# Weight slots, shared row buffers and PSUM banks in the expert stage of a hybrid decoder block

## Chip, cores and metric

The kernel runs on one NeuronCore of a Trainium2 chip. The metric is the device time of one execution in microseconds (us). What is compared are medians over several executions; lower is better.

## What is computed

One decoder block over 512 tokens of width 1024, all in float32. First comes a mixer (attention with a window, and a gated linear recurrence), then a mixture of experts, then a last norm. The change touches the expert stage alone. Cut to that stage, the reference does this:

```
logits = h @ w_router + b_router                  # 512 tokens, 32 experts
top_vals, top_idx = top_k(logits, 4); gates = softmax(top_vals)
for each expert e, for the tokens xb that chose it:
    gu   = xb @ w_gu[e] + b_gu[e]                 # 1024 -> 2 x 1024
    gate = min(gu[:, :1024], 7); up = clip(gu[:, 1024:], -7, 7)
    y    = ((up + 1) * gate * sigmoid(1.702 * gate)) @ w_down[e] + b_down[e]
    out[token] += y * gates[token, e]
```

There are 2048 pairs of a token and an expert, spread unevenly: an expert may have a few rows or some three hundred. The weights of one expert are 12 MB (8 MB of w_gu, 4 MB of w_down), 384 MB in all, and each is read from DRAM once.

## The kernel before

**Weights.** An expert's weights are loaded in 12 chunks of 1 MB, 8 of w_gu and then 4 of w_down, by SyncE's queue (`load`, L1115, issues at L1119 and L1123). A chunk lives in a slot of 128 x 2048 float32. `ORDER` (L1099) lists 20 slots; slot 19 is not among them, since it holds three other tiles (below). `pump` (L1129) issues loads while there are free slots. The 8 slots of w_gu come free when the gate and up products of that expert are done (`used(e, False)`), the 4 of w_down after its down products (`used(e, True)`). `paced` (L1105) keeps at most 4 loads under way. Before the first expert starts 18 chunks are asked for (`pump(KD + 4 + EARLY)`), and the rest of the slots are filled during the first expert.

**Experts.** One pass of the loop over e at the end of the function does, in the order of the program: the gate and up products of e (`gate_up`), the turning of the token rows of e+1 (`turn_x`, L1158), the gather of the rows of e+2 (`gather`, L1084), and the down products of e-1 (`down`). Rows are taken in tiles of 32 tokens; a tile of gate and up products is 64 matmul instructions (L1195), a tile of down products 64 (L1218). Up to four tiles are one block, and `nest` (L1166) skips tiles that an expert doesn't have, by branches on the expert's count. Experts with over 128 rows run `further`, for blocks 1 to 3.

**Down products and output.** A tile of down products goes into a PSUM bank given by `pd` (L1140), banks 4 and 5 by turns for block 0. `put` (L1221) then adds the bias (L1224, from `bd_` or for further blocks `bdx`, which `bias2` fills at L931), scales by the gate (L1225) into a row buffer `Y[:, t]`, four buffers for four tiles, and GpSimd scatters it with addition into the result in DRAM (L1226, 128 rows of 256 float32, an indirect DMA of the software queue).

**Picking rows.** For expert e+2 a one-hot tile `T_HOT` is made on VectorE (L951) right after the output of e-1, and TensorE multiplies by it between the second and the third chunk of the next gate and up products (L1068, the first step of `between`). VectorE, TensorE and GpSimd each work strictly in their own order.

**Buffers around the change.** Slot 19 holds `a4[5]` (the rows `XR` of a further block) and `a4[6]` (`bdx` in its first quarter, `T_HOT` in its second half). `a4[4]` holds `HX`, the activations of a further block, `a4[3]` the four buffers `Y`.

```
pg = lambda b, t: pall[:, 2 + t % 2 if b else t, :]
pd = lambda b, t: pall[:, (0 if b else 4) + t % 2, 0:256]
def put(e, b, t):
    si, f = INFO[e, b // 2]
    y = Y[:, t]
    V.tensor_tensor(y, pd(b, t), bdx if b else bd_, op=OP.add)
```

Of the kernel before, what the change touches and what calls it, by code (L numbers as in the profile page):

```python
# [13 lines left out]
OP = mybir.AluOpType  # L14
# [26 lines left out]
def block_kernel(ctx, tc, x, c, w_ada, b_ada, g_mix, w_in, conv_w, conv_b, w_rg_a, b_rg_a, w_rg_x,  # L41
# [3 lines left out]
    V, A, PE, G = nc.vector, nc.scalar, nc.tensor, nc.gpsimd  # L45
# [12 lines left out]
    pall = psp.tile([128, 8, 512], FT, name="pall")  # L58
# [34 lines left out]
    a4 = [wk.tile([128, D], FT, name=f"a{i}") for i in range(NA4)]  # L93
# [61 lines left out]
    btg = keep.tile([128, 768], FT, name="btg")  # L155
# [574 lines left out]
    def run_all(g):  # L730
        for _ in g:
            pass
# [182 lines left out]
    def new(name, tag=None):  # L915
        shape, dt, bufs = KINDS[name]
        return wk.tile(shape, dt, name=name, tag=tag or name, bufs=1 if tag else bufs)

    def hot_tile(at):
        return at[:, :NT * 128].bitcast(BF).rearrange("p (t n) -> p t n", t=NT)  # L920

    bd_ = wk.tile([128, 256], FT, name="bd")
    T_HOT = hot_tile(a4[6][:, 512:])
    BG = new("bg")


    def bias(e):
        V.stream_shuffle(BG, btg[:, :512], [e] * 32)  # L928

    def bias2(e, dst=bd_):  # L930
        V.stream_shuffle(dst, btg[:, 512:], [e] * 32)  # L931

    for tb in range(NT):
        assemble(tb, 0)
# [15 lines left out]
    def hot(oh, e, c, tb):  # L950
        V.tensor_scalar(oh[:, tb], slots, 256.0 * c, posm[:, tb, e:e + 1], op0=OP.add, op1=OP.is_equal)  # L951
# [86 lines left out]
    part = lambda i: a4[i].rearrange("p (t n) -> p t n", t=4)  # L1038
# [3 lines left out]
    def prep(e, c, oh, own=None, bk=5, tbs=range(NT)):  # L1042
        mk = (lambda n: own[n]) if own else new
        for tb in tbs:
            hot(oh, e, c, tb)
        yield
        where(e, c, oh, mk, bk)
        yield
        yield from spots(e, c, mk)

    def spots(e, c, mk):
        p, g1 = INFO[e, c]
        PE.matmul(p[:, 16:56], rep, g1.rearrange("p b t c -> p (b t c)"), start=True, stop=True)  # L1053
        p2 = p[:, 16:56].rearrange("p (b t c) -> p b t c", b=2, t=4)
        f, si = mk("f"), mk("si")
        V.tensor_copy(f[:, 0], p2[:, :, :, 1])  # L1056
        V.scalar_tensor_tensor(si, p2[:, :, :, 0], jcol, f[:, 0], op0=OP.add, op1=OP.add)
        V.tensor_copy(f[:, 1], p2[:, :, :, 3])
        V.tensor_tensor(f[:, 1], f[:, 1], p2[:, :, :, 2], op=OP.add)
        V.tensor_tensor(f[:, 1], f[:, 1], p2[:, :, :, 4], op=OP.add)  # L1060
        INFO[e, c] = (si, f)
        yield

    def where(e, c, oh, mk, bk):
        p = pall[:, bk, 0:56]
        for b in range(2):
            for tb in range(NT):
                PE.matmul(p[:, 5 * b:5 * b + 5], oh[:, tb, 128 * b:128 * b + 128], vals[:, tb, e, :],  # L1068
                          start=(tb == 0), stop=(tb == NT - 1))
        p3 = p[:, 0:10].rearrange("p (b c) -> p b c", b=2)  # L1070
        i1 = mk("i1")
        gi = GI[e, c] = mk("gi")
        V.tensor_reduce(i1, p3[:, :, 0:2], axis=AX.X, op=OP.add)
        V.tensor_scalar(gi, i1, 0.25, 1024.0, op0=OP.mult, op1=OP.add)
        g1 = mk("g1")
        V.tensor_tensor(g1, p3[:, :, None, :].to_broadcast([128, 2, 4, 5]),
                        tmask[:, None, :, None].to_broadcast([128, 2, 4, 5]), op=OP.mult)
        INFO[e, c] = (p, g1)

    def gather(e, b, x_, reg=None):  # L1080
        XROW[e, b] = x_

        def rows(p0, p1):
            G.indirect_dma_start(out=x_[p0:p1], out_offset=None, in_=h2_d,  # L1084
                                 in_offset=bass.IndirectOffsetOnAxis(
                                     ap=GI[e, b // 2][p0:p1, b % 2:b % 2 + 1], axis=0),
                                 bounds_check=S - 1, oob_is_err=False)

        if reg is None:
            return rows(0, 128)  # L1090
        with tc.If(reg > 128 * b + 64) as cmp:  # L1091
            rows(0, 128)
        with cmp.Else():
            with tc.If(reg > 128 * b + 32) as small:
                rows(0, 64)
            with small.Else():
                rows(0, 32)

    ORDER = (17, 14, 7, 12, 18, 11, 15, 13, 10, 9, 6, 2, 3, 4, 5, 16, 0, 8, 1, 20)  # L1099
    WG, WD = {e: [] for e in range(NE)}, {e: [] for e in range(NE)}  # L1100
    HELD, free, paces = {}, list(ORDER), []
    todo = [(e, k) for e in range(NE) for k in range(KD + 4)]
# [34 lines left out]

    pg = lambda b, t: pall[:, 2 + t % 2 if b else t, :]

    pd = lambda b, t: pall[:, (0 if b else 4) + t % 2, 0:256]  # L1140


    def xpose(e, b, xT):
        turn_x(e, b, xT)
        scale_x(e, b, xT, 0, 4)
# [68 lines left out]
    def dn(e, b, ht, t):  # L1214
        w = WD[e]
        for k in range(KD):
            for j in range(4):
                PE.matmul(pd(b, t)[32 * j:32 * j + 32], ht[:, t, 32 * k:32 * k + 32], w[k][:, j],  # L1218
                          start=(k == 0), stop=(k == KD - 1), tile_position=(0, 32 * j))

    def put(e, b, t):  # L1221
        si, f = INFO[e, b // 2]
        y = Y[:, t]
        V.tensor_tensor(y, pd(b, t), bdx if b else bd_, op=OP.add)  # L1224
        V.scalar_tensor_tensor(y, y, f[:, 1, b % 2, t:t + 1], gt2, op0=OP.mult, op1=OP.mult)  # L1225
        st = G.indirect_dma_start(out=x1_d, out_offset=bass.IndirectOffsetOnAxis(ap=si[:, b % 2, t:t + 1], axis=0),  # L1226
                                  in_=y, in_offset=None, bounds_check=S * 4 - 1, oob_is_err=False,
                                  compute_op=OP.add)
        tc.declare_no_dep(st.ins, group=f"sc{e}", reason="an expert's slots have rows of their own")
        tc.add_to_no_dep_group(f"sc{e}", st.ins)  # L1230


    H = [part(0), part(2)]
    TU, Y, HX, XR, bdx = part(1), part(3), part(4), a4[5], a4[6][:, :256]

    def gate_up(e, r, between):
        def tile(t):
# [12 lines left out]
    def down(e, r):  # L1250
        def tile(t):
            dn(e, 0, H[e % 2], t)
            put(e, 0, t)

        tile(0)
        nest(r, 0, tile, None, f"d{e}")


    def further(e, r):
        own = {n: new(n, n + "x") for n in ("g1", "i1", "gi", "f", "si")}  # L1260

        def products(t):
            gu(e, b, t)
            act(e, b, HX, t)

        def sums(t):
            dn(e, b, HX, t)
            put(e, b, t)

        def block():  # L1270
            xpose(e, b, XT[e, 0])
            if b < 3:
                with tc.If(r > 128 * b + 128):
                    if b == 1:
                        run_all(prep(e, 1, T_HOT, own, 1))
                    gather(e, b + 1, XR)
            products(0)
            nest(r, b, products)
            sums(0)
            nest(r, b, sums)  # L1280

        bias2(e, bdx)
        b = 1
        block()
        with tc.If(r > 256):
            b = 2
            block()
            with tc.If(r > 384):
                b = 3
                block()  # L1290

    pump(KD + 4 + EARLY)
# [6 lines left out]
    def second_rows(e):  # L1299
        with tc.If(G.value_load(cnt[0:1, e:e + 1], min_val=0, max_val=S) > 128):  # L1300
            gather(e, 1, XR)

    for e in range(NE):
        r = rn
        if e:
            second_rows(e)
            bias2(e - 1)
        prs = [prep(e + 2, 0, T_HOT)] if e + 2 < NE else []
        if e == 0:
            prs = [prep(u, 0, OH[u], None, bk, ()) for u, bk in ((1, 5), (0, 7), (2, 4))]  # L1310
        for pr in prs:
            next(pr)
        if e == 0:
            gates_of()

        def between():
            for pr in prs:
                next(pr, None)
            if e == 0 and (1, 0) not in XROW:
                gather(1, 0, xg)  # L1320
                second_rows(0)

                nc.sync.value_load(xg.bitcast(I32)[0:1, 0:1])
                pump()

        gate_up(e, r, between)
        used(e, False)
        if e:
            hint(rp, 32, f"d{e - 1}", 1)
        for pr in prs:  # L1330
            run_all(pr)
        if e + 1 < NE:
            rn = count(e + 1)
            bias(e + 1)
            turn_x(e + 1, 0, new("xT"))
            scale_x(e + 1, 0, XT[e + 1, 0], 0, 4)
        if e + 2 < NE:
            gather(e + 2, 0, xg, G.value_load(cnt[0:1, e + 2:e + 3], min_val=0, max_val=S))  # L1338
        if e:
            down(e - 1, rp)  # L1340
            used(e - 1, True)
        rp = r
# [59 lines left out]
```

## Time and profile before

| what | value |
|---|---|
| median of 3 runs | 1523.88 us (1520.62 to 1529.71) |
| the profiled execution, its own time | 1519.37 us |
| its span in the profile | 1517.5 us |
| TensorE matmul busy | 1226.6 us, 81% of the span |
| VectorE busy | 617.5 us, 41% |
| bytes moved by DMA | 473.02 MB, mean 312 GB/s |
| mean granted TensorE clock | 0.926 of full speed |

The rows of the prediction come from one execution, so its sums are made against 1519.37 us; that lies 4.5 us below the median. The expert stage runs from 257 us to 1495 us of the span. No engine and no queue is busy throughout: shares over the whole span say little, and what counts is which of two chains (TensorE's order, or the stream of weights) ends last in a given stretch.

### The profile page before, as it was taken

What the parts mean: (1) busy time and instruction counts of PE and PEld (TensorE: products, weight loads), DVE (VectorE), ACT (ScalarE), POOL (GpSimd) and SP (SyncE); (2) the same over time, 40 slices, a digit from 0 to 9 for tenths busy, and PEclk for the clock granted to TensorE, in tenths of its full rate; (3) what the DMA queues carried; (4) which work ended last, traced back from release to release, by engine and by line L of the source; (5) the groups of instructions that cost most, each with busy time, mean ns of one, the idle gap of its engine ahead of it and who ended that gap; (6) DMA issues with size and microseconds to landing.
All of it is one profiled execution on the core that took longest, in us unless ns stands there. A gap on an engine that the chain in (4) does not pass through costs nothing. (4 is left out here: it accounts for less than half of the span.)

```text
span 1517.5 us, 32068 instructions
## 1 busy us (share of the span) xinstructions
PE 1226.6 (81%) x12297; PEld 541.8 (36%) x12297; DVE 617.5 (41%) x1687; ACT 210.3 (14%) x467; POOL 264.1 (17%) x224
## 2 busy tenths in 40 slices
PE   6998979678888988789777688798858887879782
PEld 4655657222332433223212322352412242233331
DVE  4738856424344333333323323433422343324323
ACT  3445524100100010000000000000000000000001
POOL 3305731100120012101100200110200031011102
PEclk9998999999999999989878988999978999999997
DMA  9973158897996039989998988897998899579963
GB/s 325 334 281 102 56 233 327 352 379 306 399 388 250 10 88 406 384 337 400 391 398 330 395 360 339 310 388 305 398 394 311 364 392 405 209 286 347 401 263 124
DMA packets 94319, 473.02 MB, mean 312 GB/s; under 512 B 12888, under 2 KB 36652, under 8 KB 42764
## 3 DMA queue, kind: packets, MB, share of 16 engines
q1 hardware_dynamic: 76684, 447.39, 74.5%
q0 software_dynamic: 16928, 20.21, 6.0%
q8 instruction: 176, 2.88, 0.8%
q14 instruction: 179, 1.47, 0.2%
q10 hardware_dynamic: 352, 1.07, 0.2%
HBM read 457.78 MB, written 17.06 MB: 313 GB/s over the span
## 5 line engine op out<-in xcount | busy, mean ns | idle before, releaser
L1195 PE MATMUL pall<-wc,xT 128*32 128x512 f32 x5248 | 643.0, 635 | 131.2 <-DMA wc<-in_w_gu_dram 64.4
L1195 PEld LDWEIGHTS pall<-wc,xT 128*32 128x32 f32 x5248 | 166.3, 114 | 526.1 <-issue 414.4
L1218 PE MATMUL pall<-wc,a 128*32 128x256 f32 x5248 | 306.2, 389 | 34.2 <-DVE a L1224 19.1
L1218 PEld LDWEIGHTS pall<-wc,a 128*32 128x32 f32 x5248 | 176.0, 112 | 157.5 <-issue 29.4
L1226 POOL DMA_INDIRECT x_d<-a,si x82 | 128.2, 1563 | 409.7 <-DVE a L1225 259.0
L1206 ACT ACTIVATE a<-a 128x256 f32<-128x256 f32 x82 | 34.2, 417 | 916.0 <-DVE a L1205 916.0
L1203 DVE TENSOR_TENSOR a<-pall,bg 128x256 f32<-128x256 f32 x82 | 34.8, 425 | 275.7 <-PE pall L1195 275.7
L1084 POOL DMA_INDIRECT xg<-h_d,gi x31 | 33.0, 1064 | 634.2 <-PE pall L1158 486.5
L1158 PE MATMUL pall<-ident,xg 128*128 128x128 f32 x248 | 37.7, 301 | 53.8 <-PEq L1168 23.4
L1150 ACT ACTIVATE xT<-pall,sh2c,g2c 128x128 f32<-128x128 f32 x136 | 51.2, 456 | 214.4 <-DVEq L1171 55.4
L1224 DVE TENSOR_TENSOR a<-pall,bd 128x256 f32<-128x256 f32 x75 | 31.7, 422 | 100.8 <-PE pall L1218 95.2
L928 DVE LOAD_MASK_SELECT bg<-btg x32 | 0.4, 14 | 155.2 <-DVEq L1171 48.5
L1056 DVE COPY f<-pall 128x8 f32<-128x8 f32 x33 | 5.5, 167 | 139.3 <-PE pall L1053 139.2
L1158 PEld LDWEIGHTS pall<-ident,xg 128*128 128x128 f32 x248 | 30.2, 154 | 81.1 <-issue 81.1
L1210 DVE SCALAR_TENSOR_TENSOR a<-a 128x256 f32<-128x256 f32 x82 | 50.1, 611 | 2.8
L233 PE MATMUL pall<-hp,wp 128*128 128x512 f32 x112 | 47.3, 422 | 2.3 <-ACT hp L287 1.7
L1208 DVE TENSOR_TENSOR a<-a 128x256 f32<-128x256 f32 x82 | 34.9, 426 | 27.9 <-ACT a L1206 23.5
L234 PE MATMUL pall<-hp,wp 128*128 128x512 f32 x112 | 45.3, 405 | 0.5 <-DVE hp L289 0.5
L235 PE MATMUL pall<-hp,wp 128*128 128x512 f32 x112 | 45.0, 402 | 0.0
L1225 DVE SCALAR_TENSOR_TENSOR a<-a,f,gt 128x256 f32<-128x256 f32 x82 | 39.7, 485 | 2.9
L1212 DVE STREAM_TRANSPOSE a<-a 128x256 f32<-128x256 f32 x82 | 36.5, 445 | 2.8
L1204 DVE TENSOR_TENSOR a<-pall,bg 128x256 f32<-128x256 f32 x82 | 34.0, 415 | 0.0
(295 smaller groups left out, 1015.3 us busy)
## 6 DMA issues: line engine op xcount, KB each, us to landing
wc<-in_w_gu_dram SPq DMA_DIRECT2D x256, 1024.0 KB, 11.1
wc<-in_w_down_dram SPq DMA_DIRECT2D x128, 1024.0 KB, 11.3
wc<-in_w_ada_dram SPq DMA_DIRECT2D x24, 1024.0 KB, 8.6
wc<-in_w_in_dram SPq DMA_DIRECT2D x7, 1024.0 KB, 11.9
a<-in_x_dram SPq DMA_DIRECT2D x4, 512.0 KB, 4.5
wc<-in_w_out_dram SPq DMA_DIRECT2D x4, 512.0 KB, 6.7
wc<-in_w_out_dram SPq DMA_DIRECT2D x2, 1024.0 KB, 4.8
out_dram<-wc SPq DMA_DIRECT2D x4, 512.0 KB, 2.7
```

The source lines that it names most:

```text
L233: PE.matmul(out, ah, bh, start=start, stop=False)
L234: PE.matmul(out, ah, bl, start=False, stop=False)
L235: PE.matmul(out, al, bh, start=False, stop=stop)
L1150: A.activation(xT[:, k, :], p[:, k, :], AF.Identity, scale=g2c[:, k:k + 1], bias=sh2c[:, k:k + 1])
L1158: PE.transpose(p[:, i, :], x_[:, k * 128:(k + 1) * 128], ident)
L1195: PE.matmul(pg(b, t)[32 * j:32 * j + 32], xT[:, k, 32 * t:32 * t + 32], w[k][:, j], start=(k == 0), stop=(k == KD - 1), tile_position=(0, ...
L1208: V.tensor_tensor(ga, ga, sg, op=OP.mult)
L1210: V.scalar_tensor_tensor(hr.rearrange("p (k i) -> p i k", k=KD), by_k(up), 1.0, by_k(ga), op0=OP.add, op1=OP.mult)
L1212: V.transpose(h[:, t], hr)
L1218: PE.matmul(pd(b, t)[32 * j:32 * j + 32], ht[:, t, 32 * k:32 * k + 32], w[k][:, j], start=(k == 0), stop=(k == KD - 1), tile_position=(0, ...
L1225: V.scalar_tensor_tensor(y, y, f[:, 1, b % 2, t:t + 1], gt2, op0=OP.mult, op1=OP.mult)
L1226: st = G.indirect_dma_start(out=x1_d, out_offset=bass.IndirectOffsetOnAxis(ap=si[:, b % 2, t:t + 1], axis=0), in_=y, in_offset=None, bound ...
```

## The change

It empties slot 19 and adds it to `ORDER`, so that weights have 21 slots. For that `XR` moves into `a4[4]`, where it shares its place with `HX`; `T_HOT` moves into the second half of `a4[3]`, so that `Y` has two buffers (`t % 2`) where it had four; `bdx` is dropped, and further blocks use `bd_` too, so that `bias2(e - 1)` moves from the start of a pass to just before `down(e - 1)`. In `further` the picking and the gather of the rows of block 2 stood inside block 1, ahead of its products, and now stand behind all of block 1. Last, `pd` gives the four tiles of block 0 banks 4 to 7.

```
-    T_HOT = hot_tile(a4[6][:, 512:])
+    T_HOT = hot_tile(a4[3][:, 512:])
-    ORDER = (17, 14, 7, 12, 18, 11, 15, 13, 10, 9, 6, 2, 3, 4, 5, 16, 0, 8, 1, 20)
+    ORDER = (17, 14, 7, 12, 18, 11, 15, 13, 10, 9, 6, 2, 3, 4, 5, 16, 0, 8, 1, 19, 20)
-    pd = lambda b, t: pall[:, (0 if b else 4) + t % 2, 0:256]
+    pd = lambda b, t: pall[:, t % 2 if b else 4 + t, 0:256]
...
-        y = Y[:, t]
-        V.tensor_tensor(y, pd(b, t), bdx if b else bd_, op=OP.add)
+        y = Y[:, t % 2]
+        V.tensor_tensor(y, pd(b, t), bd_, op=OP.add)
...
-    TU, Y, HX, XR, bdx = part(1), part(3), part(4), a4[5], a4[6][:, :256]
+    TU, Y, HX, XR = part(1), part(3), part(4), a4[4]
...
         def block():
             xpose(e, b, XT[e, 0])
-            if b < 3:
-                with tc.If(r > 128 * b + 128):
-                    if b == 1:
-                        run_all(prep(e, 1, T_HOT, own, 1))
-                    gather(e, b + 1, XR)
             products(0)
...
-        bias2(e, bdx)
+        bias2(e)
         b = 1
         block()
         with tc.If(r > 256):
+            run_all(prep(e, 1, T_HOT, own, 1))
             b = 2
+            gather(e, b, XR)
             block()
...
         if e:
             second_rows(e)
-            bias2(e - 1)
...
         if e:
+            bias2(e - 1)
             down(e - 1, rp)
```

On VectorE, in a `down` of the loop, the rows before are these (L1224 and L1225 are `put`, once for each tile, L931 is `bias2`, L951 makes `T_HOT`; DMASW names a count of landed software-queue DMAs, and PE a count of TensorE's work):

```order
L1162 TENSOR_TENSOR xT<-xT,sh2c 128x512 [waits DVE_49]
L1224 TENSOR_TENSOR a_82<-pall,bd 128x256 [waits DMASW4_49,DMASW5_49,DMASW3_49,DMASW6_49,DMASW2_49,DMAHW6_49,DMASW0_49,PE_49]
...
L1224 TENSOR_TENSOR a_82<-pall,bd 128x256 [waits DMASW4_49,DMASW0_49,PE_49]
L1225 SCALAR_TENSOR_TENSOR a_82<-a_82,f,gt_882 128x256 [waits DVE_49]
L1174 COMPARE_AND_BRANCH
L1224 TENSOR_TENSOR a_82<-pall,bd 128x256 [waits DMASW5_49,DMASW1_49,PE_49]
L1225 SCALAR_TENSOR_TENSOR a_82<-a_82,f,gt_882 128x256 [waits DVE_49]
...
L931 STREAM_SHUFFLE bd<-btg 128x256 [waits DVE_49]
L951 TENSOR_SCALAR small_77<-slots,posm 128x256 x4
```

and with the change:

```order
L1162 TENSOR_TENSOR xT<-xT,sh2c 128x512 [waits DVE_49]
L931 STREAM_SHUFFLE bd<-btg 128x256 [waits DMASW2_49,DMASW0_49]
L1224 TENSOR_TENSOR a_82<-pall,bd 128x256 [waits DMASW3_49,DMASW2_49,DMASW4_49,DMASW1_49,DMASW6_49,DMASW0_49,DMASW7_49,DVE_49,PE_49]
...
L1224 TENSOR_TENSOR a_82<-pall,bd 128x256 [waits DMASW5_49,PE_49,Activation_49]
L1225 SCALAR_TENSOR_TENSOR a_82<-a_82,f,gt_882 128x256 [waits DVE_49]
L1174 COMPARE_AND_BRANCH
L1224 TENSOR_TENSOR a_82<-pall,bd 128x256 [waits DMASW6_49,PE_49]
L1225 SCALAR_TENSOR_TENSOR a_82<-a_82,f,gt_882 128x256 [waits DVE_49]
...
L951 TENSOR_SCALAR a_82<-slots,posm 128x256 x3
```

`bias2` has moved ahead of the outputs, and the one-hot tile still stands behind the last of them; the third and the fourth output now write the buffer of the first and the second, whose scatter is of the same pass.

On SyncE's queue, in a pass of the loop, the loads of weights stand like this before (branches mark where the queue passes the ends of the program's blocks):

```order
L1091 UNCONDITIONAL_BRANCH
L1119 DMA wc<-in_w_gu_dram 128x2048
L1168 UNCONDITIONAL_BRANCH
L1300 UNCONDITIONAL_BRANCH
L1119 DMA wc<-in_w_gu_dram 128x2048 x5
L1123 DMA wc<-in_w_down_dram 128x2048 x4
L1119 DMA wc<-in_w_gu_dram 128x2048
```

and with the change:

```order
L1091 UNCONDITIONAL_BRANCH
L1119 DMA wc<-in_w_gu_dram 128x2048 x2
L1168 UNCONDITIONAL_BRANCH
L1298 UNCONDITIONAL_BRANCH
L1119 DMA wc<-in_w_gu_dram 128x2048 x4
L1123 DMA wc<-in_w_down_dram 128x2048 x4
L1119 DMA wc<-in_w_gu_dram 128x2048
```

One load of w_gu has moved ahead of the block that follows: the queue stands one chunk further on than before.

On TensorE, in `further` of the first expert, block 1 begins like this before (L1158 turns its rows, L1068 and L1053 pick the rows of block 2, L1195 are its gate and up products):

```order
L1158 MATMUL pall<-ident,small_77 128x128 x8
L1273 COMPARE_AND_BRANCH
L1068 LDWEIGHTS small_77
L1068 MATMUL pall<-vals,small_77 128x5
...
L1053 MATMUL pall<-g_2221,rep 128x40
L1273 UNCONDITIONAL_BRANCH x2
L1195 MATMUL pall<-wc,xT 32x512 x32
```

and with the change:

```order
L1158 MATMUL pall<-ident,a_83 128x128 x8
L1195 MATMUL pall<-wc,xT 32x512 x32
...
L1218 MATMUL pall<-wc,a_83 32x256 x32
...
L1280 COMPARE_AND_BRANCH
L1068 LDWEIGHTS a_82
L1068 MATMUL pall<-vals,a_82 128x5
...
L1053 MATMUL pall<-g_2225,rep 128x40
L1158 MATMUL pall<-ident,a_83 128x128 x8
L1195 MATMUL pall<-wc,xT 32x512 x32
```

The picking of block 2 now stands behind the down products of block 1, directly ahead of the turning of the rows that it picks.

## Rows read from the trace of the kernel before

**Rows 1.** Waits of SyncE's queue, whole span: us in total, times, longest.
```profile
SPq L1119 <- PEq L1288: 85.1, 1, 85.1
SPq L1119 <- PEq L1178: 74.7, 7, 13.5
```

**Rows 2.** Waits of TensorE, whole span, same columns.
```profile
PE pall L1195 <- DMA wc<-in_w_gu_dram: 64.4, 45, 9.5
...
PE pall L1218 <- DVE a L1224: 19.1, 9, 2.4
```

**Rows 3.** Stretches of the span: us, busy by engine, granted clock, DMA share, GB/s.
```profile
375.00:462.00 87.00, 73.61 (x940) 32.70 (x940) 34.42 (x107) 6.60 (x17) 18.25 (x13) 0.98 1.02 385
667.00:784.00 117.00, 86.17 (x900) 32.12 (x900) 38.29 (x123) 8.11 (x21) 16.79 (x12) 0.84 1.01 390
890.00:1034.00 144.00, 130.11 (x1403) 52.79 (x1395) 53.47 (x157) 9.52 (x24) 17.13 (x12) 0.93 0.83 323
1294.00:1408.00 114.00, 96.47 (x1074) 36.71 (x1066) 40.78 (x117) 8.16 (x21) 13.29 (x9) 0.96 0.74 282
```

**Rows 4.** TensorE's waits for w_gu in 375 to 462, 561 to 646, 1208 to 1294.
```profile
PE pall L1195 <- DMA wc<-in_w_gu_dram: 0.7, 1, 0.7
...
PE pall L1195 <- DMA wc<-in_w_gu_dram: 6.0, 5, 2.0
...
PE pall L1195 <- DMA wc<-in_w_gu_dram: 5.9, 5, 1.5
```

**Rows 5.** Timeline, a `down` of four tiles: start, us, engine, line, idle before and releaser.
```profile
707.82 1.56 POOL L1226 DMA_INDIRECT x_d<-a,si  x1 [8.88 <-DVE a L1225]
...
709.69 1.55 POOL L1226 DMA_INDIRECT x_d<-a,si  x1 [0.30 <-issue]
710.80 0.42 DVE L1224 TENSOR_TENSOR a<-pall,bd 128x256 f32<-128x256 f32 x1 [2.35 <-PE pall L1218]
...
714.01 1.90 PE L1195 MATMUL pall<-wc,xT 128*32 128x512 f32 x16
714.26 0.42 DVE L1224 TENSOR_TENSOR a<-pall,bd 128x256 f32<-128x256 f32 x1 [2.51 <-PE pall L1218]
...
715.47 1.11 DVE L951 TENSOR_SCALAR small<-slots,posm 128x256 bf16<-128x256 bf16 x4
...
715.84 0.53 PE L1068 MATMUL pall<-vals,small 128*128 128x5 bf16 x3
```

**Rows 6.** Scatters, issue to landing: whole span, 967 to 970, 519 to 560.
```profile
DMA to landing us min/median/max: 3.5/9.7/13.5
...
DMA to landing us min/median/max: 8.7/9.8/11.0
...
DMA to landing us min/median/max: 3.8/3.8/4.3
```

**Rows 7.** Timeline, a `down` that starts late: second scatter and fourth output.
```profile
999.28 1.56 POOL L1226 DMA_INDIRECT x_d<-a,si  x1 [1.89 <-DVE a L1225]
...
1004.97 0.42 DVE L1224 TENSOR_TENSOR a<-pall,bd 128x256 f32<-128x256 f32 x1 [2.51 <-PE pall L1218]
```

**Rows 8.** Timeline, the expert with over 256 rows: blocks 1 and 2.
```profile
488.35 0.87 DVE L951 TENSOR_SCALAR small<-slots,posm 128x256 bf16<-128x256 bf16 x4
...
490.48 1.94 PE L1195 MATMUL pall<-wc,xT 128*32 128x512 f32 x8 [0.16 <-issue]
...
490.74 1.04 POOL L1084 DMA_INDIRECT small<-h_d,gi  x1 [33.98 <-DVE f L1056]
...
533.87 0.42 DVE L1224 TENSOR_TENSOR a<-pall,small 128x256 f32<-128x256 f32 x1 [2.51 <-PE pall L1218]
...
534.99 1.50 PE L1195 MATMUL pall<-wc,xT 128*32 128x512 f32 x12
```

**Rows 9.** DMA issues: the gathers of further blocks, count, us from issue to landing.
```profile
small<-h_d,gi POOLq DMA_INDIRECT x3, 4.3
```

**Rows 10.** Timeline, TensorE after an idle stretch of 4.5 us.
```profile
741.65 3.64 PE L1195 MATMUL pall<-wc,xT 128*32 128x512 f32 x16 [4.54 <-PEq L1171]
```

More of the change, by code (lines that the diff above doesn't have):

```diff
@@ L928, in bias, with bias2 @@
         V.stream_shuffle(BG, btg[:, :512], [e] * 32)
-    def bias2(e, dst=bd_):
-        V.stream_shuffle(dst, btg[:, 512:], [e] * 32)
+    def bias2(e):
+        V.stream_shuffle(bd_, btg[:, 512:], [e] * 32)
     for tb in range(NT):
@@ L1289, in further @@
                 b = 3
+                gather(e, b, XR)
                 block()
```

## The prediction

> **What bounds the kernel now.** I read the waits of SyncE's queue first, then those of TensorE, because the expert stage is a race of two chains: the stream of weights, which can run only as many chunks ahead as there are slots, and TensorE's work, which follows the program. In the first view [rows 1] look for SyncE waiting until a branch of `nest` or `further` is passed: these are full slots, 85.1 us once, behind the expert with over 256 rows, and 74.7 us in seven more waits. In the second [rows 2] look for the opposite, TensorE waiting for a chunk: 64.4 us in 45 waits. So each chain waits for the other in turn, and the table by stretch shows where [rows 3]: from 375 to 462 and from 667 to 784 us the DMA engines are full (share 1.0, 385 to 390 GB/s) and the weights set the time; from 890 to 1034 and from 1294 to 1408 the share is 0.83 and 0.74, and TensorE sets it. Experts with four tiles make the latter, those with one or two the former. The critical path passes from TensorE to the weights where the slots are full, and back where TensorE waits for a chunk.
>
> Six stretches are led by the weights, from the end of one full ring to the last chunk that TensorE waits for: 375 to 462, 561 to 646, 667 to 784, 806 to 890, 1034 to 1150 and 1208 to 1294; a short seventh is 1408 to 1460. How long TensorE waits in one is the slack that a later TensorE may use up there for nothing: 0.7, 6.0 and 5.9 us in the first, second and sixth [rows 4]. Of the 64.4 us that leaves 51.8 us, nearly all of it in the other three, which so have over 10 us each.
>
> **The extra slot.** The weights run one chunk further ahead in each weight-led stretch. A chunk of 1.05 MB at 390 GB/s [rows 3] is 2.7 us. It is won where the slack is larger than what the rest of the change adds to TensorE, so surely in the three long ones: 3 x 2.7 = 8.1 us. In TensorE-led stretches it is worth nothing. The stretch from 1408 has a slack of some 1.4 us: I take -1.4.
>
> **Two output buffers.** This is the large term. In the `down` of four tiles that the timeline shows [rows 5] the first two scatters are issued at 707.8 and 709.7, and the third and the fourth output start at 710.8 and 714.3, with no wait but that for TensorE. With two buffers the third output must wait until the first scatter has been read out, so until it has landed, and the fourth for the second. From issue to landing a scatter takes 9.7 us in the median, 3.5 at least and 13.5 at most [rows 6]; 8.7 and 11.0 us for the first two of another `down`, and 3.8 us only where the weights stand still, from 519 to 560. During a `down` of the loop they never stand still, because the slots of w_gu have just come free. So the fourth output would start at 709.7 + 10.4 + 0.1 = 720.2 in place of 714.3, which is **5.9 us** later (10.4 lies between the median and the 11.0 of a second scatter). With three tiles it is the third output behind the first scatter: 9.5 + 0.1 - (710.8 - 707.8) = **6.6 us**. `bias2` is moved from behind the outputs to ahead of them, and takes as much there as it leaves behind.
>
> Who waits for that: behind the outputs on VectorE stands the one-hot tile (715.5), and TensorE needs it after two chunks of the next expert (L1068 at 715.8) [rows 5]. TensorE has just come out of the 16 matmuls at 714.0, so it has nothing else to do, and stands still for the whole delay. GpSimd issues the last two scatters later, but nothing of that pass waits for them.
>
> The Trainium skill would price this differently. "DMA: Bandwidth & Descriptors", section "Anatomy of one DMA — SWDGE (gpsimd) path", fits a software-queue DMA as 2.0 us plus the bytes over 436 GB/s, which for 131 kB is an estimate of 2.3 us; by that no output would wait, and the change would gain. No row here shows a landing below 3.5 us, and under load it is 9.7 [rows 6], so the sum goes by the rows.
>
> **Which of these stalls count.** Along the timeline eleven `down`s with three or four tiles are followed by such a step. From 375 to 462 there are one of three and one of four: 6.6 + 5.9 - 0.7 of slack = +11.8. From 561 to 646 one of four: 5.9 - 6.0 = -0.1. In the three long stretches one of four each, hidden in over 10 us of slack. From 890 to 1034, TensorE-led, two of four, the second of which starts late: there the fourth output comes 5.7 us behind the second scatter [rows 7], so with a landing of 8.7 it is 3.1 us late; 5.9 + 3.1 = +9.0. From 1208 to 1294 one of four and one of three: 12.5 - 5.9 = +6.6. From 1294 to 1408 one of four: +5.9.
>
> **Four banks.** Nine times the third tile of down products waits for the first output, 19.1 us in all [rows 2]. That wait goes, but TensorE then arrives up to 2.4 us earlier at the step that waits for the one-hot tile, and only its idle time moves. I count nothing; with the buffers as before it would be worth up to 2.4 us in some passes.
>
> **The expert with over 256 rows.** In block 1 TensorE no longer waits for the picking: its products started at 490.5 [rows 8] and could start when the first part of the turned rows is scaled, at some 485.6: -4.9. Ahead of block 2 the picking now stands in the open: the last output ends at 534.8, one-hot tile to gather issue takes 490.7 - 488.4 = 2.4, the gather lands after 4.3 [rows 9], turning and scaling take 1.5, so 543 in place of 535.0 [rows 8]: +8. Together +3, between 0 and +10 if that gather took as long as a scatter under load. This is in a TensorE-led stretch.
>
> **TensorE's clock.** After 4.5 us of idle time 16 matmuls took 3.64 us [rows 10] that take 1.90 at full clock [rows 5]. Seven of the new stalls are on the path. The price is between 0 (a wait of 3 us often leaves the clock alone) and 2.3 us each, as in that place with the matmuls that follow. I take 1 us, as part of it falls into slack: +7.
>
> **The sum** is 11.8 + 3 - 0.1 - 8.1 + 9.0 + 6.6 + 5.9 - 1.4 + 7 = +33.7. On 1519.4 us of the profiled execution that is 1553; the median of the runs lies 4.5 us above it, so I forecast **1558 us**, 2.2% slower. Bounds of this case: with landings of 8.7 us and no clock cost +12 or so (each of seven stalls 1.7 us less), with landings of 12 and the full clock cost and a slow gather +60, so 1536 to 1584.
>
> **Rivals.**
> - *The outputs don't wait* (faster). If a scatter landed within the time that its buffer is free anyway, 3.0 us for the first and 4.6 for the second [rows 5], as it nearly does where the weights stand still [rows 6], only gains would be left: 2.7 us in each of five stretches with slack, 2.1 in the two short ones, some 3 for the banks, against +3 for the large expert: -15.6, so 1508 us. It decides at a landing of about 4.6 us; every `down` that I looked at under load is above 8. That is also what the fit cited above would give. Chance 8%.
> - *The stalls are mostly absorbed* (small loss). TensorE also waits at ends of branches, for up to 5 us; if a late TensorE finds that time already gone, half of each stall counts, without clock cost: 33.7 - 7 - 17 = +10, so 1534 us. Chance 14%; half of that range, near no change, I give 6%.
> - *The stalls spread* (larger loss). Each drops the clock, and the late scatters delay what waits for all landings on GpSimd, the next gather among it: +50 to +65, so 1580 us. Against it: gathers are asked for a whole pass ahead. Chance 12%.
> - *The slot is no lead.* If the queue stands at a branch all the same, 9.5 us of gain is lost: 1567 us. Against it: the extra load stands ahead of the block in SyncE's order. Chance 6%.
>
> **How the numbers follow.** The forecast has 60%. A measurement of this kernel can tell about 0.5%, 7.6 us, from no change. Faster by more: the first rival, 8%. Within: 6%, out of the second. Slower: the rest, 86%. The range leaves out the first rival and the top of the third: 1530 to 1582 us.
>
> **What would show it.** In the profile of the changed kernel: VectorE L1224 waiting for the scatter (the DMA of x_d), about two waits in each of nine `down`s of four tiles and one in those of three, 3 to 8 us each; TensorE L1068 waiting for L951 with several times its 10.9 us; no wait of L1218 for L1224; SyncE's full slots still there, one chunk later; TensorE's waits for w_gu shorter in the long stretches. The prediction is wrong if scatters land in under 5 us in those `down`s, or if TensorE's wait moves elsewhere without the time growing.

## The result, and the profile after

| | before | after |
|---|---|---|
| median | 1524.23 us (1520.62 to 1529.71, 4 runs) | 1568.04 us (1564.19 to 1573.43, 4 runs) |
| the profiled execution, its own time | 1519.37 us | 1564.19 us |
| its span | 1517.5 us | 1562.4 us |
| TensorE matmul busy | 1226.6 us | 1231.1 us |
| mean granted TensorE clock | 0.926 | 0.911 |
| DMA, mean | 312 GB/s | 303 GB/s |

The change makes the kernel slower: the ratio is 1.0287, with an interval of 1.024 to 1.0334. The forecast was 1558 us. TensorE is busy for only 4.5 us more while the span grows by 44.9 us, so most of the loss is time in which TensorE stands still.

The view to read first is that of the waits, here of VectorE and TensorE (engine, tile and line, what it waited for: us in total, times, longest). Kernel before, whole span, the two rows that matter most:

```profile
PE pall L1068 <- DVE small L951: 10.9, 17, 4.0
...
DVE a L1224 <- DMA x_d<-a,si: 2.5, 1, 2.5
```

and the kernel after:

```profile
DVE a L1224 <- DMA x_d<-a,si: 125.5, 22, 9.8
...
PE pall L1068 <- DVE a L951: 92.6, 20, 9.0
...
PE pall L1195 <- DMA wc<-in_w_gu_dram: 26.0, 19, 7.3
...
PE pall L1195 <- DMA wc<-in_w_down_dram: 13.6, 6, 5.6
...
PE pall L1218 <- DVE a L1224: 2.8, 1, 2.8
```

VectorE's wait for a scatter was a single one of 2.5 us before: now it waits 22 times until a scatter has landed and its output buffer is free, 5.7 us each. The second row after the change is what this does to TensorE, which waits 92.6 us for the one-hot tile; the same step waited 10.9 us before. In turn TensorE's wait for w_gu has fallen from 64.4 us [rows 2] to 26.0, because a TensorE that is late finds its weights there. The wait of L1218 for the first output, 19.1 us [rows 2], has shrunk to a single one of 2.8 us.

The other chain, the same view for SyncE's queue of the kernel after, against [rows 1]:

```profile
SPq L1119 <- PEq L1285: 97.5, 1, 97.5
SPq L1119 <- PEq L1178: 79.1, 7, 23.2
```

The full slots are all still there: 97.5 us where it was 85.1, and 79.1 where it was 74.7. The weights wait a little longer for a TensorE that is later.

One `down` of four tiles in the timeline (start, us, engine, line and operation, in brackets the idle time before and its releaser), kernel after. It answers to [rows 5]:

```profile
862.37 1.58 POOL L1226 DMA_INDIRECT x_d<-a,si  x1 [5.70 <-DVE a L1225]
...
864.26 1.56 POOL L1226 DMA_INDIRECT x_d<-a,si  x1 [0.31 <-DVE a L1225]
...
871.60 0.42 DVE L1224 TENSOR_TENSOR a<-pall,bd 128x256 f32<-128x256 f32 x1 [7.61 <-DMA x_d<-a,si]
...
874.81 0.42 DVE L1224 TENSOR_TENSOR a<-pall,bd 128x256 f32<-128x256 f32 x1 [2.27 <-DMA x_d<-a,si]
...
875.67 0.87 DVE L951 TENSOR_SCALAR a<-slots,posm 128x256 bf16<-128x256 bf16 x4
...
876.01 0.89 PE L1068 MATMUL pall<-vals,a 128*128 128x5 bf16 x8 [7.52 <-DVE a L951]
...
876.83 5.32 PE L1195 MATMUL pall<-wc,xT 128*32 128x512 f32 x32
```

Read it from the top. The first scatter is issued at 862.37; the third output, which writes the same buffer, starts 9.2 us later. The fourth follows the second scatter by 10.6 us, and only then comes the one-hot tile, 13.3 us behind the first scatter; in the `down` of [rows 5] it was 7.65 us (715.47 - 707.82). So the tile comes 5.65 us later, and TensorE has stood still for 7.52 us. The last row shows the second price: these 32 matmuls took 5.32 us here. Their counterparts before, after a `down` of four tiles:

```profile
426.68 3.64 PE L1195 MATMUL pall<-wc,xT 128*32 128x512 f32 x32
```

and after, at the same place in the program and after a `down` late in the span:

```profile
441.78 6.09 PE L1195 MATMUL pall<-wc,xT 128*32 128x512 f32 x32
...
1263.63 6.46 PE L1195 MATMUL pall<-wc,xT 128*32 128x512 f32 x32
```

The table by stretch (columns as in [rows 3]) puts the clock beside it, before:

```profile
422.00:442.00 20.00, 18.51 (x189) 6.47 (x182) 8.49 (x30) 0.83 (x2) 3.46 (x3) 1.00 1.04 383
```

and after, the same work:

```profile
430.00:460.00 30.00, 19.92 (x177) 6.47 (x169) 9.11 (x30) 0.83 (x2) 3.98 (x3) 0.83 0.74 268
```

Before, the granted clock was 1.00 there (2.4 GHz). After, TensorE stood still for 9 us and then had 0.83 over the stretch, so part of its work ran at the lower level of 1.2 GHz. The DMA share fell from 1.04 to 0.74: the stretch has gone over from the weights to TensorE.

**Where the time went, by stretch.** The timelines of both profiled executions were laid side by side at the start of each turning of rows (L1158) or product (L1195, L1218). The forecast has here the 1 us for the clock in each stall counted.

| stretch of the kernel before | forecast | measured |
|---|---|---|
| 375 to 440, two stalls | +13.8 | +17.6 |
| 440 to 561, expert with over 256 rows | +3 | +5.2 |
| 561 to 668 | -0.1 | +0.1 |
| 668 to 807, weight-led | -2.7 | +0.3 |
| 807 to 915, weight-led | -2.7 | -1.8 |
| 915 to 1036, two stalls | +11.0 | +10.2 |
| 1036 to 1175, weight-led | -2.7 | -2.7 |
| 1175 to 1318, two stalls | +8.6 | +6.2 |
| 1318 to 1409, one stall | +6.9 | +13.8 |
| 1409 to the end | -1.4 | -3.7 |
| sum | +33.7 | +45.2 |

### The profile page after: what moved, and what is told of

It reads as the page before. It is cut to its first block, busy times and chain, and to the rows that moved or that the text cites. A ratio compares the mean times of both kernels' runs of the same rounds, so it can differ in the third digit from the quotient of the medians.

```text
span 1562.4 us, 32100 instructions
## 1 busy us (share of the span) xinstructions
PE 1231.1 (79%) x12297; PEld 538.8 (34%) x12297; DVE 618.9 (40%) x1687; ACT 210.3 (13%) x467; POOL 264.0 (17%) x224
## 5 line engine op out<-in xcount | busy, mean ns | idle before, releaser
L1195 PE MATMUL pall<-wc,xT 128*32 128x512 f32 x5248 | 648.3, 644 | 104.4 <-ACT xT L1150 26.2
L1195 PEld LDWEIGHTS pall<-wc,xT 128*32 128x32 f32 x5248 | 169.3, 116 | 499.3 <-issue 427.3
L1218 PE MATMUL pall<-wc,a 128*32 128x256 f32 x5248 | 302.8, 389 | 16.6 <-ACT xT L1150 7.5
L1218 PEld LDWEIGHTS pall<-wc,a 128*32 128x32 f32 x5248 | 169.0, 112 | 144.5 <-issue 21.9
L1203 DVE TENSOR_TENSOR a<-pall,bg 128x256 f32<-128x256 f32 x82 | 34.8, 425 | 250.8 <-PE pall L1195 250.3
L1224 DVE TENSOR_TENSOR a<-pall,bd 128x256 f32<-128x256 f32 x82 | 34.8, 425 | 166.6 <-DMA x_d<-a,si 125.5
L1068 PE MATMUL pall<-vals,a 128*128 128x5 bf16 x240 | 19.4, 173 | 95.1 <-DVE a L951 92.6
L1150 ACT ACTIVATE xT<-pall,sh2c,g2c 128x128 f32<-128x128 f32 x136 | 51.2, 456 | 238.8 <-DVEq L1168 74.7
L1158 PE MATMUL pall<-ident,xg 128*128 128x128 f32 x248 | 36.8, 295 | 50.4 <-PEq L1171 9.1
L1068 PEld LDWEIGHTS <-a 128*128 128x128 bf16 x240 | 12.5, 101 | 137.7 <-DVE a L951 116.2
L1158 PEld LDWEIGHTS pall<-ident,xg 128*128 128x128 f32 x248 | 29.4, 151 | 75.8 <-issue 56.7
L1225 DVE SCALAR_TENSOR_TENSOR a<-a,f,gt 128x256 f32<-128x256 f32 x82 | 39.8, 485 | 2.9
## 6 DMA issues: line engine op xcount, KB each, us to landing
wc<-in_w_in_dram SPq DMA_DIRECT2D x7, 1024.0 KB, 10.6
```

The lines of the kernel that those rows point to most:

```text
L1150: A.activation(xT[:, k, :], p[:, k, :], AF.Identity, scale=g2c[:, k:k + 1], bias=sh2c[:, k:k + 1])
L1158: PE.transpose(p[:, i, :], x_[:, k * 128:(k + 1) * 128], ident)
L1195: PE.matmul(pg(b, t)[32 * j:32 * j + 32], xT[:, k, 32 * t:32 * t + 32], w[k][:, j], start=(k == 0), stop=(k == KD - 1), tile_position=(0, ...
L1203: V.tensor_tensor(ga, p[:, 0:256], BG[:, 0:256], op=OP.add)
```

## The experiments

All ratios are to the kernel before on the same chip, with a 95% interval. Times of parts below are ratio differences times 1524 us.

**1. The two output buffers alone.** The kernel before, with one line changed:

```diff
-        y = Y[:, t]
+        y = Y[:, t % 2]
```

> The kernel before with one edit: two output buffers in place of four. Theory (the third and fourth output wait for a scatter to land, the one-hot tile stands behind them on VectorE, and TensorE waits for it): the whole loss and more, since the extra slot gives nothing back: 1565 to 1585 us, VectorE L1224 waiting some 125 us for the scatter in about 22 waits, TensorE L1068 waiting 80 us or more for L951. Rival (the loss comes from the rest of the sharing: rows with activations, the later gather, the moved bias): within 10 us of 1524.

Measured: 1567.25 us, ratio 1.0271 (1.0238 to 1.0303). Its waits:

```profile
DVE a L1224 <- DMA x_d<-a,si: 121.1, 21, 10.1
...
PE pall L1068 <- DVE small L951: 72.6, 27, 7.1
...
PE pall L1195 <- DMA wc<-in_w_gu_dram: 30.5, 22, 8.0
...
PE pall L1218 <- DVE a L1224: 21.6, 9, 2.5
```

So this one line costs +41 us, nearly as much as the whole change, and it makes the same rows: VectorE's wait for scatters, TensorE's at L1068 (72.6 us, a little under the 80 that were expected).

**2. The one-hot tile ahead of the outputs.** The changed kernel, with the tile of expert e+3 made before the outputs of e-1, so that TensorE's step does not stand behind them:

```diff
+        if e and e + 3 < NE:
+            ahead[e + 3] = prep(e + 3, 0, T_HOT)
+            next(ahead[e + 3])
+            begun.add(e + 3)
         if e:
             bias2(e - 1)
             down(e - 1, rp)
```

> The changed kernel with the one-hot tile made ahead of the outputs on VectorE in place of behind them. Two output buffers stay, so VectorE still waits 100 us or more for scatters. Theory: what costs is only what stands behind that wait, so TensorE's wait at L1068 falls below 30 us and the time to 1515 to 1540 us; some is left, because the next step on VectorE (L1073, for L1053) is still behind the outputs. Rival (any wait of VectorE of that size costs its time, whatever stands behind it): above 1555.

Measured: 1538.17 us, ratio 1.0105 (1.0055 to 1.0156), so about two thirds of the loss are gone. The waits:

```profile
DVE a L1224 <- DMA x_d<-a,si: 108.9, 19, 9.0
...
PE pall L1053 <- DVE g L1076: 53.9, 12, 5.9
...
PE pall L1068 <- DVEq L1168: 10.6, 5, 2.7
...
PE pall L1068 <- DVE a L951: 1.3, 1, 1.3
```

VectorE still waits for scatters almost as long (108.9 us where it was 125.5), but TensorE's wait for the one-hot tile at L1068 is down from 92.6 to 1.3 us. It meets the late VectorE one step on, at L1053, whose operand `g` VectorE makes behind the outputs. A late engine is worth what stands next behind it: moving the first step on TensorE's path out of the way leaves the second.

**3. Four output buffers and the slot.** The changed kernel, with the one-hot tile in the scratch of the activations, so that the outputs have their four buffers and the weights keep 21 slots:

```diff
-    T_HOT = hot_tile(a4[3][:, 512:])
+    T_HOT = hot_tile(a4[1][:, :512])
...
-        y = Y[:, t % 2]
+        y = Y[:, t]
```

> The changed kernel with four output buffers again: the one-hot tile moves to the scratch of the activation (free while the tile is in use), 21 slots, four banks and shared rows stay. Theory: no wait of L1224 for the scatter, L1068 back near 11 us, and only the gains of slot and banks and the +4 of the large expert are left: 1503 to 1522 us. Rival (the rest of the sharing costs): above 1545.

Measured: 1514.6 us, ratio 0.994 (0.9908 to 0.9972): faster than either kernel. Its waits:

```profile
PE pall L1195 <- DMA wc<-in_w_gu_dram: 58.7, 47, 8.5
...
PE pall L1068 <- DVE a L951: 8.1, 5, 2.2
```

VectorE waits for a scatter only once, 1.8 us. With TensorE on time, its wait for w_gu is back.

**4. The changed kernel with 20 slots** (slot 19 left out of `ORDER`).

```diff
-    ORDER = (17, 14, 7, 12, 18, 11, 15, 13, 10, 9, 6, 2, 3, 4, 5, 16, 0, 8, 1, 19, 20)
+    ORDER = (17, 14, 7, 12, 18, 11, 15, 13, 10, 9, 6, 2, 3, 4, 5, 16, 0, 8, 1, 20)
```

> The changed kernel with 20 slots (slot 19 empty and unused). Theory: the extra slot gave 2.7 us in each of the stretches with slack, so 6 to 14 us slower than the change: 1574 to 1582 us. Rival (the slot is no lead, or its lead is lost within the stretch): within 3 us of 1568.

Measured: 1580.85 us, ratio 1.0369 (1.0336 to 1.0401). The slot gives 12.5 us in the changed kernel; with the intervals of both ratios that is some 4 to 21 us. But here is a sum that did not close: this kernel and that of experiment 1 both have 20 slots and two buffers, and stand 15 us apart. Some other part costs about that much. The experiments 5 to 8 look for it.

**5 to 7. The banks.** Three kernels: the one before with four banks, the changed one with the two banks of before, and that of experiment 1 with four banks.

```diff
-    pd = lambda b, t: pall[:, (0 if b else 4) + t % 2, 0:256]
+    pd = lambda b, t: pall[:, t % 2 if b else 4 + t, 0:256]
```

> The kernel before with nothing changed but four banks for the down products. My prediction: the waits of L1218 for L1224 (19.1 us, nine times) go, TensorE arrives up to 2.4 us earlier at L1068 and waits there for the one-hot tile instead, so between 0 and -5 us on some 1523 us: a ratio of 0.997 to 1.000. Rival, the whole 19.1 us is on the path in TensorE-led stretches: 1510 us or less. Second rival, the banks cost something (TensorE runs ahead and its clock falls at the longer wait): 1526 us or more.

> The changed kernel with the two alternating banks of the kernel before. Without the extra slot the changed kernel takes 1580.9 us, but the kernel before with two output buffers alone 1567.3 us, though both have 20 slots: some 13 us are lost by another part. Theory: the four banks. They bring TensorE up to 2.4 us earlier to the step that waits for the late one-hot tile, so it stands still longer in one piece (7.5 instead of 6.2 us) and its clock falls further; then this kernel takes 1555 to 1561 us, ratio 1.020 to 1.025. Rival: the banks are worth nothing and the loss lies in the late picking and in bias2 ahead of the outputs: 1566 to 1570 us, ratio 1.027 to 1.031, with the wait at L1068 shorter by as much as L1218 waits longer.

> The kernel before with two output buffers and four banks, nothing else. If four banks harm beside two buffers: 1573 to 1580 us, ratio 1.032 to 1.037, against 1.027 with two buffers alone. If they are worth nothing: 1565 to 1569 us, ratio 1.026 to 1.029, with the 21.6 us that L1218 waits for L1224 moved to L1068.

Measured: before with four banks 1523.21 us, ratio 0.999 (0.9975 to 1.0006); the changed kernel with two banks 1571.12 us, 1.0298 (1.0271 to 1.0325), against 1.0287 with four; two buffers with four banks 1567.14 us, 1.0261 (1.0235 to 1.0288), against 1.0271 with two. In no pair can the banks be told from nothing, and the theory that they do harm beside two buffers has fallen. With two output buffers the reason is seen in the waits, of the changed kernel with two banks:

```profile
PE pall L1068 <- DVE a L951: 61.2, 16, 6.2
PE pall L1218 <- DVE a L1224: 35.3, 12, 3.5
```

and of two buffers with four banks:

```profile
PE pall L1068 <- DVE small L951: 88.8, 26, 8.7
```

The sum of the two waits is 96.5 us with two banks and, in the kernel after, 92.6 + 2.8 us with four; in experiment 1 it is 72.6 + 21.6 = 94.2 us, against 88.8 + 2.5 here. The wait only changes its line. With four output buffers it is not so. The kernel before with four banks has

```profile
PE pall L1068 <- DVE small L951: 13.2, 17, 4.0
```

so of the 16.5 us that L1218 no longer waits only 2.3 have come back at L1068, and the expected move did not happen. What grew is TensorE's busy time, from 1226.6 to 1236.9 us, at a granted clock of 0.916 where it was 0.926; why the clock is lower there is not shown.

**8. The late picking and gather alone.** The kernel before, with the picking and the gather of a further block moved behind the block ahead of it:

```diff
-            if b < 3:
-                with tc.If(r > 128 * b + 128):
-                    if b == 1:
-                        run_all(prep(e, 1, T_HOT, own, 1))
-                    gather(e, b + 1, XR)
...
         with tc.If(r > 256):
+            run_all(prep(e, 1, T_HOT, own, 1))
             b = 2
+            gather(e, b, XR)
             block()
...
```

> The kernel before with the picking and the gather of the rows of a further block moved behind the block ahead of it, nothing else. My prediction: block 1 of the expert with over 256 rows starts 4.9 us earlier, block 2 some 8 us later against it, +3 us together: 1525 to 1530 us, ratio 1.001 to 1.004. Rival, the late gather holds the next experts back too (the part of the loss that the slots and the buffers don't explain): +10 us or more, ratio 1.007 and above.

Measured: 1535.25 us, ratio 1.0071 (1.0049 to 1.0094), or +11 us: not the forecast but the rival, and most of the missing part. The timeline of TensorE shows the piece that had been forecast:

```profile
514.66 14.00 PE L1218 MATMUL pall<-wc,a 128*32 128x256 f32 x256
530.26 0.57 PE L1068 MATMUL pall<-vals,small 128*128 128x5 bf16 x3 [1.60 <-DVE small L951]
...
536.87 1.97 PE L1158 MATMUL pall<-ident,small 128*128 128x128 f32 x8 [4.76 <-DMA small<-h_d,gi]
```

Block 1 starts 4.9 us earlier, block 2 is 8.3 us later against it, and at 561 us the kernel is +4.8 us behind. Another 3.4 us come at the next expert with a second block, at 1338: its down products, 64 matmuls, took 3.66 us before and 5.07 here, the same work at a lower clock (granted 0.71 where it was 1.00), and the turning behind them waits longer. In the kernel after it is the same place and the same way:

```profile
1363.73 5.35 PE L1218 MATMUL pall<-wc,a 128*32 128x256 f32 x64 [3.16 <-DVE a L1212]
...
1376.63 1.94 PE L1158 MATMUL pall<-ident,xg 128*128 128x128 f32 x8 [7.55 <-DMA xg<-h_d,gi]
```

The next expert's first products lose about as much again in both kernels (their first 16 matmuls take 3.6 us where they took 1.9), so that between 1318 and 1358 us 6.7 us are lost here and 5.9 in the kernel after.

The traces and runs say two things more of this loss. First, it shows in the clock and not in waiting: TensorE's busy time in the profiled execution is

```profile
PE 1244.2 (81%) x12297; PEld 540.0 (35%) x12297; DVE 618.0 (40%) x1687; ACT 210.2 (14%) x467; POOL 263.7 (17%) x224
```

or 17.6 us more than before, while the span is 15.0 us longer; over all runs of the experiment the granted clock is 0.9125 in the mean, against 0.922 in the runs of the kernel before beside them. Second, it goes with the late gather: in all ten kernels here that have it the stretch from 1318 to 1358 us is 3.8 to 7.0 us longer than before, and in the three that don't 0.2 to 1.4 us. Why the clock is lower there, behind a wait of 3.2 us that was as long before, is not settled.

**9. Fewer loads under way.** The changed kernel, with two weight loads under way at most. Nothing but the pace of the loads differs.

```diff
-DEPTH = 4
+DEPTH = 2
```

> The changed kernel with at most two weight loads under way where it had four. It tells why a scatter takes 9 us to land. Theory: a scatter queues behind the weight loads that are already under way, 4.2 MB or 10.8 us at 390 GB/s; with half of that the median landing falls to 5 or 6 us, and VectorE's wait of L1224 for the scatter from 125.5 to below 60 us. What the time does depends on whether two loads keep the engines full: 1540 us if they do, over 1570 if they don't. Rival, the scatter is slow in itself (accumulation, 128 descriptors by software): the landing stays at 8 to 10 us and the wait above 110 us.

Measured: 1614.29 us, ratio 1.0566 (1.0524 to 1.0608). Landing of the scatters (from issue; us; against [rows 6]), in the kernel after:

```profile
DMA to landing us min/median/max: 3.4/9.0/11.7
```

in its stretch from 532 to 560 us, where the weights stand still:

```profile
DMA to landing us min/median/max: 3.6/3.7/3.8
```

and with two loads under way, whole span:

```profile
DMA to landing us min/median/max: 3.6/6.3/11.0
```

with these waits:

```profile
DVE a L1224 <- DMA x_d<-a,si: 94.0, 21, 6.5
...
PE pall L1068 <- DVE a L951: 60.0, 17, 7.2
...
PE pall L1195 <- DMA wc<-in_w_gu_dram: 100.1, 62, 11.1
```

The direction is that of the theory: with half of the loads under way the median landing falls from 9.0 to 6.3 us. So a scatter is slow because of the loads, and not in itself. But it does not simply queue behind them, as the theory had it. By the packets of the trace the first scatter of the `down` shown above, issued at 862.37, starts to move its 128 rows at 866.8 and lands at 871.5, and between the two some 190 packets of 1 KB, of this scatter and the next, run among some 180 of 8 KB of the weights. Where the weights stand still, the rows of a scatter start 2.1 us after its issue and take 1.1 us. So the scatter shares the DMA engines with the loads. The size is less than expected: 6.3 us lies just above the 5 to 6, and VectorE's wait fell to 94.0 us, not below 60. The time is lost for another reason: two loads do not feed TensorE, which now waits 100.1 us for w_gu.

**10 to 12. What the better version is made of.** The version of experiment 3, once with the old two banks, once with the picking back inside block 1 (only the gather stays late), once with 20 slots. The first and the last by the lines of experiments 5 and 4; the second:

```diff
             xpose(e, b, XT[e, 0])
+            if b == 1:
+                with tc.If(r > 256):
+                    run_all(prep(e, 1, T_HOT, own, 1))
             products(0)
...
-            run_all(prep(e, 1, T_HOT, own, 1))
             b = 2
```

> The changed kernel with four output buffers and with the two alternating banks of the kernel before. It tells what of the gain of the version with four buffers and four banks (1514.6 us, ratio 0.994) is the slot's and what the banks'. If the banks are worth nothing: the same ratio, 0.993 to 0.996. If they are the gain and the slot is none: 1523 us, ratio 1.000. The waits of L1218 for L1224, 19 to 22 us in nine, come back in either case.

> The changed kernel with four output buffers, the one-hot tile in the activation scratch, and the picking of block 2 of the large expert back in block 1; only the gather of its rows stays behind block 1, since they share a place with the activations. Block 1 starts 4.9 us later than with the picking behind it, and block 2 starts 2.4 to 4 us earlier, so it should stand within 2 us of the version with four buffers: 1512 to 1517 us, ratio 0.992 to 0.996. Rival, the late gather is the whole price and the picking none: 1511 us.

> The version with four output buffers and four banks, with 20 slots: what is left of the change then is the late picking and gather and the place of bias2. The parts measured so far add up to the change: two buffers +43, late picking and gather +11.5, banks 0, slot -13, together +42 of +44 us. If they add up here as well: 1524 + 11.5 = 1535 us, ratio 1.007, and the slot would have given 21 us in the version with four buffers. Rival: the late picking and gather cost less in this version, whose XR lies elsewhere: 1526 to 1529 us, ratio 1.001 to 1.004, and the slot is worth the same 13 us in both.

Measured: two banks 1520.15 us, ratio 0.9964 (0.9946 to 0.9982); picking back 1516.09 us, 0.9946 (0.992 to 0.9972); 20 slots 1540.36 us, 1.0094 (1.0069 to 1.0118). Neither the picking nor the banks make a difference that the intervals tell apart. The last is the telling one. It came out 5 us above the 1535 that the parts add up to, and with four buffers the slot is worth (1.0094 - 0.994) x 1524 = 23 us (some 17 to 30), where it gives 12.5 (4 to 21) beside two; that it is worth more here is likely, but the intervals still overlap. Laid side by side, the version with 21 slots is ahead of that with 20 by 4.6 us at 483 us of the kernel before, 9.4 at 668, 17.4 at 1034 and 24 at 1300, so it keeps gaining; in the changed kernel the same lead (against experiment 4) stays within some 3 us of nothing up to 860 us and is 10 at 1460. Of the 28 us between the profiled executions with four buffers 18.6 are TensorE's busy time (1229.3 against 1247.9 us): without the slot it does not so much wait longer as work at a lower clock (0.917 against 0.908 in the mean of the runs).

## Why the prediction was right, and where its sizes were off

**What bounds the kernel, and the chain of the stall: right.** The wait for a scatter appears on L1224 of VectorE, 22 times, where I had forecast about two for each `down` of four tiles and one for each of three, 3 to 8 us each (5.7 in the mean, 9.8 at most). It reaches TensorE at L1068, behind the one-hot tile. Experiment 1 shows it alone: one line, +41 us. Experiment 2 shows that the order on VectorE carries it on: with the tile ahead of the outputs two thirds of the loss go.

**Two output buffers, +33.2 us and +7 for the clock: right to 1 us, +41 measured, in part by luck.** By the step that came first, a landing of 10.4 us for the second scatter, the fourth output would follow that scatter by 10.5 us; in the `down` shown it is 10.55, and its one-hot tile is 5.65 us later where 5.9 had been forecast. But taken from ahead of the `down` to behind the wait, the seven stalls cost 5.7 to 8.6 us each, 48 us in all, where the prediction had 39.9 us before slack. The one that was forecast at 3.1 us, because its `down` starts late, cost as much as the others (TensorE's delay goes from 22.9 to 30.2 us there): its first two scatters now stood 1.9 us apart, where [rows 7] had been read with the spacing of before. Stalls and clock were both larger than forecast, and slack took back more.

**The clock, 1 us for each stall: too small.** The 32 matmuls behind the seven stalls took 5.14, 6.09, 4.92, 5.05, 6.46, 5.07 and 5.82 us where they take 3.64; one such place was known [rows 10]. That is 13.1 us, 1.9 us each, near the upper end of the bound (2.3). At the sixth of these places the kernel before had spent 5.80 us too, waits included, so that against that kernel the seven come to 10.9 us. That the stalls with their clock yet came out at +41 fits with slack that took some of it back.

**The extra slot, -9.5 us: right in sign, -12.5 measured** beside two buffers. It runs one chunk further ahead, as said: at the same full ring the queue stood before the fifth chunk of an expert (794.4 to 805.7 us), and now stands before the sixth (818.2 to 828.9). From 668 to 807 us, though, the lead of 2.7 us was gone by the end of the stretch (+0.3), with a DMA share of 0.97 over it in both kernels; what took it I did not settle. I had priced the slot by one chunk in each long stretch; the 12.5 us agree with that within their interval, and with four buffers it is worth 23 us, most of it in a clock that the sum had not tied to the slot.

**Four banks, 0: right**, in four pairs of kernels. The reason given, that TensorE's idle time moves to L1068, holds in the two pairs with two output buffers, which is the case that the prediction was about; with four buffers it does not (experiment 5).

**The expert with over 256 rows, +3 us: mis-sized, and the main error of the sum: +11 measured.** In the stretch itself it was nearly right: -4.9 and +8 were forecast for its two halves from [rows 8, 9], and -4.9 and +7.9 came in the kernel after; +5.2 with the neighbours. What was missed is the second expert with two blocks, at 1318 us, for which the prediction had no term: the stretch from 1318 to 1409 came out at +13.8 for +6.9, and 3.1 us of it lie between 1318 and the turning at 1338, 5.9 up to 1358. This term had counted starts and waits, and experiment 8 shows that what it costs is mostly work at a lower clock.

**The sum.** Measured one by one: buffers +41, late picking and gather +11, banks 0 (-1.5 by the single comparison), slot -12.5, together +39.5; the change as a whole is +43.7. Forecast: +40.2, +3, 0, -9.5, together +33.7. The parts so explain the result to within some 4 us, which is less than their intervals. The lower bound of the prediction is added up wrongly: seven stalls of 1.7 us less and no clock cost leave +15 and not +12, so 1539 in place of 1536 us.

**The rivals.** That outputs don't wait has fallen: a landing of 4.6 us was the point from which it decides, and the least in the kernel after is 3.4, the median 9.0. The Trainium skill's "DMA: Bandwidth & Descriptors", section "Anatomy of one DMA — SWDGE (gpsimd) path", by which a landing was an estimate of 2.3 us, is not borne out here: 3.7 us with the weights standing, 9.0 with four loads under way. That the stalls are mostly absorbed has fallen by experiment 1. That they spread, +50 to +65, is nearer, since the clock did cost almost its upper bound: the measured +43.7 (37 to 51) lies between the forecast and this rival. That the slot is no lead has fallen by experiments 4 and 12.

## What to carry to other kernels

A buffer that is handed to a transfer is taken until that transfer has landed, and what a landing takes is read beside the traffic of the same stretch, not beside idle queues. Before two buffers are shared, look at what stands behind the writer on its own engine: here a wait of some 10 us for a scatter cost TensorE 7.5 us and 1.9 us of lower clock, because the tile that it needs next is made behind the output. And a gain in one chain (a slot more for the weights) is worth what the other chain leaves of it: the same slot gave 12.5 us beside late outputs and 23 us beside punctual ones (with intervals that overlap), so give up for it the space whose users have time (here the one-hot tile goes into the scratch of the activations), not the buffers of a slow transfer. Last, look at an engine's busy time as well as at its waits: the late gather and the missing slot cost more in matmuls at a lower clock than in idle time.

## What the runs showed of the hardware

- A scatter of 128 rows of 1 KB lands after 3.7 us where the weights stand still, after 6.3 us in the median with two loads of 1 MB under way, and after 9.0 us with four. It shares the DMA engines with the loads, though it comes from another queue: beside four loads its 1 KB packets run among their 8 KB packets, some 190 and 180 between 866.8 and 871.5 us of the kernel after.
- With two loads of 1 MB under way in place of four, the mean is 293 GB/s in place of 303, TensorE's wait for w_gu 100.1 in place of 26.0 us, and the time 1614 in place of 1568 us.
- After an idle time of 7.4 to 9 us TensorE took 4.9 to 6.5 us for 32 matmuls that take 3.64 us at full clock, at each of the seven stalls counted. After one of 3.2 us the same 64 matmuls (at 1328 us of the kernel before) took 3.66 us in eight of the fourteen kernels and 5.07 to 6.58 us in the other six; what decides there I did not find.
